# Linear attention of heads 0 and 1 interleaved with the gate projections, on other SBUF addresses, with the decays kept on chip

## The chip, the cores and the metric

One NeuronCore of a Trainium2 chip runs the whole kernel. The metric is the device time of one execution, in microseconds (us). An execution is also profiled; its trace gives the start and the length of every instruction on the engines: PE (matrix multiply; PEld is its weight load), DVE (vector), ACT (activation), POOL (GpSimd) and SP, whose queue issues nearly all DMAs here.

## The reference

A two-layer backbone over 256 context tokens and 1024 latent tokens, 1024 wide. Layer 0 is attention. Layer 1, where the change lies, runs two mixers side by side on the same normalized input `h`, and a SwiGLU block after them:

```python
q, k, v, g, lr, zg, zx = split(h @ w_in)              # 4 heads: q, k 64 wide, v 128 wide; g 512; zg, zx 512
log_a = log_sigmoid(lr @ gate_w + gate_b) / 16        # one decay for each head, key channel and direction
# linear attention, forward and backward in time, context first and then latent:
#   S <- exp(sum of log_a) * S + (k decayed to the block's end)^T v
#   o =  (q decayed from the block's start) S  +  the products inside the block
y_gla = rms_norm(o_forward + o_backward) * silu(g)    # g is the output gate
y_lru = (gated linear recurrence of conv(zx), both directions) * gelu(zg)
x = x + gate1 * (concat(y_gla, y_lru) @ w_out)
```

## The kernel before

All projections are transposed: 128 output channels on the partitions, tokens on the free axis in three chunks of 256, 512 and 512 (the first is the context). A product in float32 is made of three matmuls of split operands, so a 128-wide projection of all 1280 tokens is 72 matmuls on PE (8 blocks of the input, 3 products, 3 chunks). The code is written in program order; a planner with its own cost model puts each engine's instructions into one fixed order, near to program order, in which it lets ready work fill gaps that it foresees. On the chip each engine and the SP queue work that list strictly in order. Memory is handed out from pools that grow from the left or from the right end of SBUF; a tile that takes over the place of an older one waits until everything that uses the older tile is done.

`layer1` (L1679) runs a list of steps, `L1A` and then `L1B` (L54, L55). A letter is a kind of step and the digit the head or the group of 128 channels:

- `z` (`proj_zg`, L1348), `k` (`proj_t`, keys and queries of one head, 64 rows each), `x` (`proj_t` of the recurrence's input), `v` (`proj_v`, L1517, values, turned token-major by PE transposes L1527; its last chunk is turned in a later step) and `g` (`proj_g`, L1488, output gates of latent tokens, two chunks of 24 matmuls, then a Tanh on ACT, L1494, and a product on DVE, L1495). Their results go to DRAM through a ring of four tiles, `st`.
- `l` (`lru`, L1364): the recurrence of one group: convolution and gelu, 24 gate matmuls (L1390), activations, and scans on DVE (L1404, L1407, L1408). Its tile `ti` has one buffer.
- `a` (`gla_gates`, L1430): 6 small matmuls (L1438), Abs, Exp and Ln on ACT (L1440 to L1442) and the log decay `z` on DVE (L1443), which is stored to DRAM as `dz`.
- `p` (`gla_prep`, L1446): for each of the three chunks it loads `z` (L1461), keys over queries and queries over keys (L1457 to L1459), takes running sums `c` of `z` in blocks of 128 tokens (L1464, DVE), and makes from Exps of differences the decayed keys (POOL, L1479 and L1480, 64 rows each) and, for latent chunks, the decayed queries (DVE, L1484 and L1485, 64 rows each). Its tiles have one buffer, so a chunk's loads wait for the chunk before. `c`, the second sum `v` and both products go to DRAM.

When all steps are done, the pools of layer 1 and the one of `h` close, and the linear attention begins in the place of `h`, at the left end. For each head `gla_states` (L1551) loads decayed keys and values, makes the states of 8 blocks (PE transposes L1565, products L1571, a chain of 16 updates on DVE, L1583), and `gla_half` (L1586) does the first 512 latent tokens in 7 levels: two differences on POOL (L1620, L1621), an Exp on ACT (L1622), three products on DVE (two `kx` of 64 rows, L1627, and `qx`, L1628), 4 products on PE (L1632) and a masked copy on DVE (L1634). Then come the output products (L1639, L1640), a norm and the product with the gate. `gla_setup` (L1541) loads the masks and clears seven tiles for head 0. `out1` (L1666), the output projection, two rounds of 96 matmuls for the half of the input that comes from the recurrence, stands behind head 2 and behind head 3 in program order; its input (`y1_load`) and the residual tiles `x` are loaded behind head 0. The other 512 tokens of each head come later, inside the SwiGLU block.

Of the kernel before, what the change touches and what calls it, by code (L numbers as in the profile page):

```python
# [53 lines left out]
L1A = ops("z0 k0 l0 z1 k1 a0 l1 a1 z2 k2 a2 l2 a3")  # L54
L1B = ops("x3 z3 p0 k3 l3 p1 v0 p2 v1 v2 p3 v3 g0 g1 g2 g3")  # L55
# [84 lines left out]
class Trunk:  # L140
# [1000 lines left out]
    def layer0(self):  # L1141
# [165 lines left out]
        return h2, h2x, l1x  # L1307
# [8 lines left out]
    def proj(self, m, h, chunks, name):  # L1316
        w = self.wload(self.a["w1"][m], f"w1_{m}")
        for ci in chunks:
            cn = CH[ci][1]
            pt = self.psum(f"{name}{m}_{ci}", BANKS)  # L1320
            self.mm3(pt[:, 0:cn], w, h[ci], KT, lambda k: (slice(None), slice(k * P, (k + 1) * P)), lambda k: (slice(None), k))
            yield ci, pt[:, 0:cn]
# [107 lines left out]
    def gla_gates(self, pool, m):  # L1430

        nc = self.nc
        z = pool.tile([P, NTOK], F32, tag="pz", bufs=1, name=f"pz{m}")
        e = pool.tile([P, NTOK], F32, tag="pe", bufs=1, name=f"pe{m}")
# [9 lines left out]
        nc.sync.dma_start(self.dz[m], z)  # L1444

    def gla_prep(self, pool, m):  # L1446

        nc = self.nc
        for ci, (c0, cn) in enumerate(CH):
# [3 lines left out]
            def tl(tag, bufs=1):  # L1453
                return pool.tile([P, 512], F32, tag=tag, bufs=bufs, name=f"{tag}{nm}")[:, 0:cn]

            kq, qk = tl("pkq"), tl("pqk")
            nc.sync.dma_start(kq, self.dkq[m][:, sl])  # L1457
            nc.sync.dma_start(qk[0:64], self.dkq[m][64:128, sl])
            nc.sync.dma_start(qk[64:128], self.dkq[m][0:64, sl])  # L1459
            z, c, e = tl("pz"), tl("pc"), tl("pf")  # L1460
            nc.sync.dma_start(z, self.dz[m][:, sl])  # L1461
# [12 lines left out]
            ea, eb = e, tl("pb")  # L1474
            nc.gpsimd.tensor_tensor(v3(eb), ends.unsqueeze(2).to_broadcast([P, nt, P]), v3(z), op=ALU.subtract)
            nc.scalar.activation(ea, z, AF.Exp, scale=1.0 / 16)
            nc.scalar.activation(eb, eb, AF.Exp, scale=1.0 / 16)
            kh = tl("pk")
            nc.gpsimd.tensor_tensor(kh[0:64], kq[0:64], eb[0:64], op=ALU.mult)  # L1479
            nc.gpsimd.tensor_tensor(kh[64:128], qk[64:128], ea[64:128], op=ALU.mult)  # L1480
            nc.sync.dma_start(self.dkt[m][:, sl], kh)
            if ci:
                qh = c
                nc.vector.tensor_tensor(qh[0:64], qk[0:64], ea[0:64], op=ALU.mult)  # L1484
                nc.vector.tensor_tensor(qh[64:128], kq[64:128], eb[64:128], op=ALU.mult)  # L1485
                nc.sync.dma_start(self.dqh[m][:, c0 - C:c0 - C + cn], qh)

    def proj_g(self, h, pool, m):  # L1488

        nc = self.nc  # L1490
        for ci, pt in self.proj(4 + m, h, (1, 2), "g"):
# [4 lines left out]
            nc.sync.dma_start(self.dsg[m][:, c0:c0 + 512], st)  # L1496

# [19 lines left out]
    def proj_v(self, h, pool, m):  # L1517
# [4 lines left out]
        def turn(f, ci):  # L1522
# [7 lines left out]
            nc.sync.dma_start(self.dv[:, t0:t0 + nt, m * P:(m + 1) * P], st[:, 0:cn].rearrange("p (t c) -> p t c", c=P))  # L1530
# [10 lines left out]
    def gla_setup(self, pool):  # L1541
# [7 lines left out]
        self.st = {(h, 1): pool.tile([P, 4, P], F32, name=f"S1{h}") for h in range(4)}  # L1549

    def gla_states(self, pool, h, setup=None):  # L1551

        nc = self.nc
        kh = pool.tile([P, NTOK], F32, tag="kh", bufs=1, name=f"kh{h}")
        nc.sync.dma_start(kh, self.dkt[h])
        vh = pool.tile([P, 10, P], F32, tag="vs", bufs=2, name=f"vs{h}")
        nc.sync.dma_start(vh, self.dv[:, :, h * P:(h + 1) * P])
        if setup:
            setup()
        dec = self.dec[:, h]  # L1560
        u = []
        for g, (t0, tn) in enumerate(((0, 4), (4, 4), (8, 2))):
            pt = self.psum(f"kt{h}_{g}", "bb")
            for j in range(tn):
                nc.tensor.transpose(pt[:, j * P:(j + 1) * P], kh[:, (t0 + j) * P:(t0 + j + 1) * P], self.ident)  # L1565
            kt = pool.tile([P, 512], F32, tag="kt", bufs=2, name=f"kt{h}_{g}")
            self.evac(kt[:, 0:tn * P], pt[:, 0:tn * P])
            pu = self.psum(f"pu{h}_{g}")
            for j in range(tn):
                t = t0 + j  # L1570
                nc.tensor.matmul(pu[:, j * P:(j + 1) * P], kt[:, j * P:(j + 1) * P], vh[:, t], start=True, stop=True)  # L1571
                u.append(pu[:, j * P:(j + 1) * P])
# [13 lines left out]
    def gla_half(self, pool, h, half, tags="bbc"):  # L1586
# [18 lines left out]
        nc.sync.dma_start(vh, self.dv[:, 2 + half * 4:6 + half * 4, h * P:(h + 1) * P])  # L1605
# [73 lines left out]
    def layer1(self, h, h2x, l1):  # L1679
# [3 lines left out]
        self.dv = self.dp.tile([P, 10, 512], F32, name="dv")  # L1683
# [5 lines left out]
        self.dz = [self.dp.tile([P, NTOK], F32, name=f"dz{m}") for m in range(4)]  # L1689
# [5 lines left out]
        lp = lx.enter_context(self.pool("l1", "right"))  # L1695
        later = []

        def stages(todo, pp):
            for op, m in todo:
                turn = None  # L1700
# [317 lines left out]
```

## Time and profile before

| | us |
|---|---|
| median of 3 runs | 3202.02 |
| lowest and highest | 3200.45, 3204.18 |
| the profiled execution | 3202.41 |
| its span, first to last instruction | 3200.6 |

The span is the part of an execution that the trace shows; 1.8 us of the profiled execution lie around it. PE is busy 2927.1 us, DVE 2143.7, ACT 1278.9 and POOL 1258.3. Matmuls overlap one another, so that a busy PE is not yet a PE at its peak.

### The profile page before, as it was taken

The numbers are of one execution on the slowest core, as the hardware profiler recorded it, in microseconds if no ns is written. First come the engines' busy times: TensorE is split into PE (matmuls) and PEld (weight loads), VectorE is DVE, ScalarE is ACT, GpSimd is POOL, SyncE is SP. The second block draws the span as 40 slices with busy tenths as digits, with TensorE's granted clock in tenths as the row PEclk, the third lists the DMA queues.
The fourth block names the chain that finished last, engine by engine and source line by source line (L and its number), as shares of the span: only waits on it lengthen the run. The fifth ranks groups of instructions, "written<-read, shape, count | busy, mean of one in ns | idle before, by whom it ended". The sixth has DMA issues, their size and how long they took to land. (4 is left out here: it accounts for less than half of the span.)

```text
span 3200.6 us, 40905 instructions
## 1 busy us (share of the span) xinstructions
PE 2927.1 (91%) x14936; PEld 2396.7 (75%) x14936; DVE 2143.7 (67%) x3621; ACT 1278.9 (40%) x1971; POOL 1258.3 (39%) x741
## 2 busy tenths in 40 slices
PE   7998899998979999999989999886889999999997
PEld 5986677876768888888877766665667777787876
DVE  5598878885786555556687456647867665655487
ACT  4311655653442222324443367422333332333343
POOL 2333432332243333235445322444545434343455
PEclk9999999998989999999999999997989999999999
DMA  6576433315424444447423322567323233222452
GB/s 247 176 241 202 114 91 100 90 30 189 159 85 153 151 151 154 140 148 283 145 83 112 109 79 85 172 185 227 123 80 106 76 105 91 94 102 100 148 191 99
DMA packets 217193, 433.31 MB, mean 135 GB/s; under 512 B 23392, under 2 KB 91744, under 8 KB 216736
## 3 DMA queue, kind: packets, MB, share of 16 engines
q1 hardware_dynamic: 212384, 413.93, 40.3%
q10 hardware_dynamic: 4608, 16.78, 1.8%
q8 instruction: 117, 1.92, 0.2%
q14 instruction: 84, 0.69, 0.1%
HBM read 323.01 MB, written 107.61 MB: 135 GB/s over the span
## 5 line engine op out<-in xcount | busy, mean ns | idle before, releaser
L264 DVE SCALAR_TENSOR_TENSOR adaw<-adaw,cr 128x1024 f32<-128x1024 f32 x96 | 140.8, 1466 | 88.9 <-DMA adaw<-adat 88.7
L764 POOL TENSOR_TENSOR l_fx<-r_fin,h_fx 128x1024 fp32r<-128x1024 f32 x36 | 88.7, 2463 | 264.1 <-ACT h_fx L763 264.1
L764 POOL TENSOR_TENSOR l_fw<-r_fin,h_fw 128x1024 fp32r<-128x1024 f32 x36 | 87.4, 2428 | 168.0 <-ACT h_fw L763 148.3
L538 POOL TENSOR_SCALAR s_d<-s_d,cf_d 128x1280 f32<-128x1280 f32 (+1 forms) x40 | 46.6, 1164 | 248.3 <-DVE nb_d L525 63.6
L518 PE MATMUL ps_d<-kd,q 128*128 128x512 f32 (+1 forms) x416 | 116.5, 387 | 18.5 <-DVE s_d L520 13.4
L200 POOL TENSOR_TENSOR l_w<-r_w,h_w 128x1024 fp32r<-128x1024 f32 x33 | 85.0, 2578 | 95.0 <-ACT h_w L199 85.0
L520 DVE TENSOR_SCALAR_CACHE_REDUCE s_d<-ps_d 128x512 f32<-128x512 f32 (+1 forms) x208 | 117.1, 580 | 6.4 <-PE ps_d L518 5.1
L876 DVE TENSOR_TENSOR r_fin<-r_fin,r_fin 128x512 f32<-128x512 f32 x36 | 24.9, 692 | 132.1 <-POOL l_fx L764 131.9
L364 PE MATMUL pq<-hhi,h_w 128*128 128x512 f32 (+1 forms) x312 | 111.1, 356 | 1.5 <-DVE yl L435 1.5
L364 PE MATMUL pq<-hlo,h_w 128*128 128x512 f32 (+1 forms) x312 | 112.1, 359 | 0.0
L364 PE MATMUL pq<-hhi,l_w 128*128 128x512 f32 (+1 forms) x312 | 111.3, 357 | 0.0
L1632 PE MATMUL pg<-qx,kx 128*128 128x128 f32 x448 | 73.8, 318 | 31.0 <-DVE qx L1628 30.3
L539 POOL TENSOR_TENSOR s_d<-s_d,s_d 128x1280 f32<-128x1280 f32 (+1 forms) x40 | 99.7, 2493 | 3.3
L531 ACT ACTIVATE s_d<-s_d,nb_d 128x1280 f32<-128x1280 f32 (+1 forms) x80 | 94.5, 1183 | 14.5 <-DVE nb_d L526 8.8
L962 POOL TENSOR_TENSOR bl<-r_b,bh 128x1024 fp32r<-128x1024 f32 (+2 forms) x32 | 65.5, 2055 | 86.4 <-ACT bh L961 83.9
L1632 PEld LDWEIGHTS pg<-qx,kx 128*128 128x128 f32 x448 | 66.3, 224 | 41.6 <-issue 25.5
L518 PEld LDWEIGHTS ps_d<-kd,q 128*128 128x128 f32 x416 | 68.4, 194 | 34.6 <-DVE s_d L520 20.2
L962 POOL TENSOR_TENSOR bl_0t<-r_b0t,bh_0t 128x1024 fp32r<-128x1024 f32 (+1 forms) x24 | 70.0, 2924 | 61.3 <-ACT bh_0t L961 61.3
L432 POOL TENSOR_TENSOR rsh<-rsh,rope 128x512 f32<-128x512 f32 x26 | 41.3, 1590 | 133.4 <-DVE rsh L429 95.2
L364 PE MATMUL pd<-bh,h_fo 128*128 128x512 f32 (+1 forms) x228 | 84.7, 373 | 5.0 <-DVE xz L1018 2.7
L814 ACT ACTIVATE et<-es 128x512 f32<-128x512 f32 x54 | 34.0, 631 | 137.1 <-DVE es L887 68.4
L328 DVE TENSOR_TENSOR nacc<-nacc,nsq 128x512 f32<-128x512 f32 (+1 forms) x77 | 75.3, 981 | 20.0 <-ACT nsq L327 17.9
(625 smaller groups left out, 10405.4 us busy)
## 6 DMA issues: line engine op xcount, KB each, us to landing
r_fin<-fin SPq DMA_DIRECT2D x104, 512.0 KB, 3.6
adaw<-adat SPq DMA_DIRECT2D x64, 512.0 KB, 3.7
q<-dq SPq DMA_DIRECT2D x160, 128.0 KB, 3.0
r_w<-w SPq DMA_DIRECT2D x33, 512.0 KB, 3.8
adaw<-adat ACTq DMA_DIRECT2D x32, 512.0 KB, 4.8
r_wo<-wo SPq DMA_DIRECT2D x32, 512.0 KB, 3.8
w<-fo SPq DMA_DIRECT2D x32, 512.0 KB, 6.6
dbt<-et SPq DMA_DIRECT2D x44, 256.0 KB, 2.5
```

Of the source, the lines that this page charges most:

```text
L200: eng.tensor_tensor(lo, raw, hi.bitcast(F32), op=ALU.subtract)
L264: nc.vector.scalar_tensor_tensor(o, w, 1.0, cs[v], op0=ALU.mult, op1=ALU.mult, accum_out=self.adac[l][:, m, v:v + 1])
L328: nc.vector.tensor_tensor(acc, acc, sq, op=ALU.add)
L364: nc.tensor.matmul(out, w[wi][wsl(k)], x[xi][xsl(k)], start=(first and k == 0 and i == 0), stop=(last and k == nk - 1 and i == 2), skip_gr ...
L518: nc.tensor.matmul(pt[:, 0:kn], q[:, m, ab, j * P:(j + 1) * P], kt[:, m, k0:k0 + kn], start=(ab == 0), stop=(ab == 1))
L520: nc.vector.tensor_scalar(s[m][:, k0:k0 + kn], pt[:, 0:kn], 1.0, None, op0=ALU.mult, op1=ALU.max, accum_out=mx[:, m, c:c + 1])
L531: nc.scalar.activation(s[m][:, 0:nk * P], s[m][:, 0:nk * P], AF.Exp, bias=nb[:, m:m + 1], scale=SC, accum_out=sm[:, m:m + 1])
L538: nc.gpsimd.tensor_scalar(a1, a1, cf, 0.0, op0=ALU.mult, op1=ALU.add)
L539: nc.gpsimd.tensor_tensor(a0, a0, a1, op=ALU.add)
L764: eng.tensor_tensor(lo[:, 0:n], raw[:, 0:n], hi[:, 0:n].bitcast(F32), op=ALU.subtract)
L962: eng.tensor_tensor(lo[:, 0:n], raw, hi[:, 0:n].bitcast(F32), op=ALU.subtract)
L1632: nc.tensor.matmul(pg[:, b], kx[:, b], qx[:, b], start=True, stop=True)
```

## The change

1. One list `L1` takes the place of `L1A` and `L1B`: values and preparation (`v`, `p`) stand between the recurrences, and the `g` steps leave the list. The ring `st` and the tiles of `a` and `p` get pools at the left (`stp`, `pp`).
2. `a` keeps `z` in SBUF (`self.z`), in one buffer until its `p` has read it; `dz` is gone, its store and its loads too. The scratch tile of `a` is now the recurrence's `ti`.
3. `p` loads keys twice and queries twice (forward and backward rows), and forms both exponents as 128-row tiles whose halves hold the two directions; decayed keys and decayed queries are one Exp and one product of all 128 rows each. The decayed keys take a slot of the ring `st`. The second sum is stored as two halves of 64 rows.
4. Values lie in DRAM as one tensor for each head.
5. The working tiles of the linear attention (`gp`, `gh`) move to the right end, where the recurrence's tiles were; heads 0 and 1 take their decayed keys, values and states from four tiles in the pool of `h` that held the normalized context tokens (`WT[2][0:4]`). `h` thus stays, and the `g` steps are interleaved with heads 0 and 1: three steps of the heads, then one chunk of a gate.
6. The residual tiles and the later pools move to the left; `x` and the first `y1_load` come behind head 1, and `out1` behind heads 2 and 3.

```diff
-L1A = ops("z0 k0 l0 z1 k1 a0 l1 a1 z2 k2 a2 l2 a3")
-L1B = ops("x3 z3 p0 k3 l3 p1 v0 p2 v1 v2 p3 v3 g0 g1 g2 g3")
+L1 = ops("z0 k0 l0 k1 z1 v0 l1 a0 p0 z2 k2 v1 l2 a1 p1 x3 z3 k3 v2 l3 a2 p2 v3 a3 p3")
...
-    def gla_gates(self, pool, m):
+    def gla_gates(self, pool, lp, m):
-        z = pool.tile([P, NTOK], F32, tag="pz", bufs=1, name=f"pz{m}")
-        e = pool.tile([P, NTOK], F32, tag="pe", bufs=1, name=f"pe{m}")
+        self.z = z = pool.tile([P, NTOK], F32, tag="pz", bufs=1, name=f"pz{m}")
+        e = lp.tile([P, NTOK], F32, tag="ti", bufs=1, name=f"pe{m}")
...
-        nc.sync.dma_start(self.dz[m], z)
...
+            kk, qq = tl("pkq"), tl("pqk")
+            for i, t in enumerate((kk, qq)):
+                if i == 0 or ci:
+                    for r in (lo, hi):
+                        nc.sync.dma_start(t[r], self.dkq[m][64 * i:64 * i + 64, sl])
+            z, c = self.z[:, sl], tl("pc")
...
+            ka, qa = tl("pf"), tl("pb")
+            nc.vector.tensor_tensor(ka[hi], c[hi], z[hi], op=ALU.subtract)
+            nc.scalar.activation(qa[lo], c[lo], AF.Copy)
...
-            nc.gpsimd.tensor_tensor(kh[0:64], kq[0:64], eb[0:64], op=ALU.mult)
-            nc.gpsimd.tensor_tensor(kh[64:128], qk[64:128], ea[64:128], op=ALU.mult)
+            for r, t, v in ((lo, ka, c), (hi, qa, ka)):
+                nc.gpsimd.tensor_tensor(v3(t[r]), ends[r].unsqueeze(2).to_broadcast([64, nt, P]), v3(v[r]), op=ALU.subtract)
+            kh, qh = tl("st", sp, 4), c
+            nc.scalar.activation(kh, ka, AF.Exp, scale=1.0 / 16)
+            nc.gpsimd.tensor_tensor(kh, kh, kk, op=ALU.mult)
             nc.sync.dma_start(self.dkt[m][:, sl], kh)
             if ci:
-                nc.vector.tensor_tensor(qh[0:64], qk[0:64], ea[0:64], op=ALU.mult)
-                nc.vector.tensor_tensor(qh[64:128], kq[64:128], eb[64:128], op=ALU.mult)
+                nc.scalar.activation(qh, qa, AF.Exp, scale=1.0 / 16)
+                nc.vector.tensor_tensor(qh, qh, qq, op=ALU.mult)
...
     def proj_g(self, h, pool, m):
-        for ci, pt in self.proj(4 + m, h, (1, 2), "g"):
+        for ci, pt in self.proj(4 + m, h, (1, 2), "g", "ad"):
...
             nc.sync.dma_start(self.dsg[m][:, c0:c0 + 512], st)
+            yield
...
+        gp, gh = [gx.enter_context(self.pool(n, "right")) for n in ("gp", "gh")]
+        gates = chain(*[self.proj_g(h, stp, m) for m in range(4)])
+        next(gates)
+        for turn in later:
+            turn()
+        def heads():
+            for hd in range(2):
+                t = [hb.tile([P, 1024], F32, tag=tag, bufs=1, name=f"gl{hd}{i}") for i, tag in enumerate(WT[2][0:4])]
+                self.gla_states(((t[0], t[3][:, 0:256]), (v3(t[1]), v3(t[3][:, 256:512])), (t[2][:, 0:512], t[2][:, 512:1024]),
+                                 self.st[3, 1] if hd else v3(t[3][:, 512:1024])), hd, None if hd else lambda: self.gla_setup(gp))
+                yield from self.gla_half(gh, hd, 0)
+        weave(heads(), gates, 3)
         h2x.close()
...
+            y = self.y1_load(yp, 1, 1)
+            for ci in (1, 2):
+                c0 = CH[ci][0] - C
+                for k in range(KT):
+                    nc.sync.dma_start(x[ci][:, k], self.dx[:, k, c0:c0 + 512])
+            for hd in (2, 3):
+                self.gla_states(self.gla_tiles(pool, hd), hd)
                 run(self.gla_half(gh, hd, 0))
+                run(self.out1(y, x, 1, hd - 1, "ad"))
+                if hd == 2:
                     y = self.y1_load(yp, 1, 2)
```

## Rows read from the trace of the kernel before

**Rows 1.** Stretches: length, busy PE, PEld, DVE, ACT, POOL (instructions), clock, DMA share, GB/s.
```profile
1839.50:2010.50 171.00, 160.17 (x650) 116.60 (x649) 102.51 (x85) 114.34 (x132) 44.65 (x28) 0.94 0.26 89
2010.50:2107.50 97.00, 76.91 (x349) 60.83 (x348) 54.62 (x58) 42.02 (x69) 46.47 (x30) 0.89 0.55 171
2107.50:2151.80 44.30, 44.30 (x199) 36.35 (x197) 23.81 (x30) 14.65 (x28) 20.52 (x15) 1.00 0.60 188
2151.80:2163.30 11.50, 0.04 (x2) 0.05 (x1) 5.54 (x5) 2.15 (x4) 8.70 (x10) 0.66 0.72 241
2163.30:2308.70 145.40, 112.52 (x609) 94.87 (x610) 116.96 (x216) 47.96 (x74) 74.23 (x76) 0.82 0.57 175
2308.70:2334.00 25.30, 22.29 (x97) 17.72 (x96) 14.59 (x23) 8.61 (x12) 13.64 (x11) 0.87 0.42 132
```

**Rows 2.** Timeline of PE, last gate to first level: start, length, instruction, [idle before, releaser].
```profile
2151.43 0.39 PE L364 MATMUL g<-h,h_w 128*128 128x512 f32 x1
2163.28 2.51 PE L1565 MATMUL kt<-ident,kh 128*128 128x128 f32 x10 [11.46 <-DMA kh<-dkt]
2176.51 0.77 PE L1632 MATMUL pg<-qx,kx 128*128 128x128 f32 x2 [5.48 <-DVE qx L1628]
```

**Rows 3.** Timeline of the SP queue, and of POOL, at the same place.
```profile
2157.14 0.41 SPq L1496 DMA_DIRECT2D dsg<-stg  x1
2157.65 0.38 SPq L1555 DMA_DIRECT2D kh<-dkt  x1
2164.27 0.38 SPq L1595 DMA_DIRECT2D C<-dc  x1
...
2170.90 0.62 POOL L1620 TENSOR_TENSOR D<-C,V 128x256 f32<-128x256 f32 x1 [10.40 <-DMA C<-dc]
```

**Rows 4.** Waits from 2151.8 to 2334: who waited for whom, us, times, longest.
```profile
POOL D L1620 <- DVE qx L1628: 32.9, 12, 8.4
PE pg L1632 <- DVE qx L1628: 28.5, 18, 5.5
```

**Rows 5.** Waits from 1839.5 to 2151.8.
```profile
DVE pc L1464 <- DMA pz<-dz: 45.0, 9, 8.5
PE vt L1527 <- ACT vf L1534: 13.9, 4, 5.0
```

**Rows 6.** Timeline of PE: projection k3, then the gate matmuls of recurrence 3.
```profile
1996.69 0.28 PE L364 MATMUL kq<-h,h_w 128*128 128x256 f32 x1
...
2010.47 4.46 PE L1390 MATMUL lg<-xr,r_lg 128*128 128x256 f32 x12
2021.10 6.81 PE L1390 MATMUL lg<-xr,r_lg 128*128 128x256 f32 x12 [6.17 <-DVE stkq L1314]
```

**Rows 7.** Timelines: first gate matmul of recurrence 0; last scans of recurrences 0 and 3.
```profile
1864.21 8.75 PE L1390 MATMUL lg<-xr,r_lg 128*128 128x256 f32 x24
1891.59 2.34 DVE L1408 TENSOR_TENSOR_SCAN lq<-av,lq,ti 128x1024 f32<-128x1024 f32 x1
2048.56 2.64 DVE L1408 TENSOR_TENSOR_SCAN lq<-av,lq,ti 128x1024 f32<-128x1024 f32 x1
```

**Rows 8.** Timelines of ACT and DVE: the decay of head 0.
```profile
1904.75 1.28 ACT L1440 ACTIVATE pe<-pz 128x1280 f32<-128x1280 f32 x1
1910.96 1.49 DVE L1443 SCALAR_TENSOR_TENSOR pz<-pz,pe 128x1280 f32<-128x1280 f32 x1 [7.05 <-ACT pe L1442]
```

**Rows 9.** Lines one by one: count, shortest/median/longest ns, first and last start.
```profile
L1464 DVE TENSOR_TENSOR_SCAN pc<-ones,pz x40: 391/398/2360, 2006.6 to 2147.1; 128x128 f32<-128x128 f32 x40
L1479 POOL TENSOR_TENSOR pk<-pkq,pb x12: 717/1604/2604, 2010.7 to 2150.9; 64x512 f32<-64x512 f32 x8, 64x256 f32<-64x256 f32 x4
L1484 DVE TENSOR_TENSOR pc<-pqk,pf x8: 683/1712/2786, 2016.9 to 2151.2; 64x512 f32<-64x512 f32 x8
L1485 DVE TENSOR_TENSOR pc<-pkq,pb x8: 1648/1669/4037, 2018.7 to 2152.8; 64x512 f32<-64x512 f32 x8
L1628 DVE TENSOR_TENSOR qx<-qk,D x30: 669/693/2108, 2175.7 to 2311.8; 128x512 f32<-128x512 f32 x30
```

More of the change, by code (lines that the diff above doesn't have):

```diff
@@ L1306, in layer0 @@
         fx.close()
-        return h2, h2x, l1x
+        return h2, hb, h2x, l1x
     def evac(self, dst, src, i=1):
@@ L1564, in gla_states @@
             for j in range(tn):
-                nc.tensor.transpose(pt[:, j * P:(j + 1) * P], kh[:, (t0 + j) * P:(t0 + j + 1) * P], self.ident)
-            kt = pool.tile([P, 512], F32, tag="kt", bufs=2, name=f"kt{h}_{g}")
+                nc.tensor.transpose(pt[:, j * P:(j + 1) * P], key(t0 + j), self.ident)
+            kt = kts[g % 2]
             self.evac(kt[:, 0:tn * P], pt[:, 0:tn * P])
@@ L1682, in layer1 @@
         self.dy = [self.dp.tile([P, T], F32, name=f"dy{i}") for i in range(8)]
-        self.dv = self.dp.tile([P, 10, 512], F32, name="dv")
+        self.dv = [self.dp.tile([P, 10, P], F32, name=f"dv{i}") for i in range(4)]
         self.dc = [self.dp.tile([P, T], F32, name=f"dc{i}") for i in range(4)]
@@ L1722, in layer1 @@
-        with self.pool("pg") as pp:
-            stages(L1A, pp)
-        stages(L1B, l1.enter_context(self.pool("pp")))
-        l1.close()
+        for op, m in L1:
+            turn = None
+            if op == "x":
+                self.proj_t(h, stp, 12 + m, self.dzx[m], f"zx{m}")
+            elif op == "k":
+                self.proj_t(h, stp, m, self.dkq[m], f"kq{m}")
+            elif op == "z":
+                self.proj_zg(h, lp, m)
+            elif op == "v":
+                turn = self.proj_v(h, stp, m)
+            elif op == "a":
+                self.gla_gates(pp, lp, m)
+            elif op == "p":
+                self.gla_prep(pp, stp, m)
+            else:
+                self.lru(lp, m)
+            if op in "vkxz" and later:
+                later.pop()()
+            if turn:
+                later.append(turn)
@@ L1726, in layer1 @@
+        weave(heads(), gates, 3)
         h2x.close()
-        lx.close()
-        ctx0, gx = ExitStack(), ExitStack()
-        gp, gh = [gx.enter_context(self.pool(n)) for n in ("gp", "gh")]
-        xp = ctx0.enter_context(self.pool("xp1", "right"))
+        ctx0 = ExitStack()
+        xp = ctx0.enter_context(self.pool("xp1"))
         def xtiles(name):
@@ L1760, in layer1 @@
         prs, ps = {}, {}
-        with self.pool("o1", "right") as pool:
+        with self.pool("o1") as pool:
             run(self.out1(self.y1_load(pool, 0, 1, sc), x, 0, 1, BANKS))
```

121 lines of the change are left out of this document (42 added, 79 removed).

## The prediction

> **What bounds the kernel now.** I read the page's busy shares first: PE is busy 2927 of 3200.6 us, so time is lost only where PE stands idle or runs at the lower of its two clock levels. A table of stretches then finds the place [rows 1]. In layer 1 up to the end of the gates (1839.5 to 2151.8) PE idles 10.8 us in the first stretch (171.0 less 160.2), 20.1 in the second and nothing in the third; the mean granted clock of 0.94 in the first means that it ran at 1.2 instead of 2.4 GHz for about 12% of the time, which costs 6% of 171, some 10 us. Then come 11.5 us with no PE work at all. The linear attention with the interleaved output projection (145.4 us to the last head's output products) has PE busy 112.5 us at a clock of 0.82, and a tail of 25.3 us.
>
> The timeline of PE names the empty 11.5 us: the last gate matmul starts at 2151.43, the first transpose of head 0 at 2163.28, released by the load of the decayed keys, and the first level's product follows at 2176.51 [rows 2]. In the SP queue that load stands behind a gate store that waits for its data and goes at 2157.14; the last tile the levels need, `C`, is issued at 2164.27, and POOL begins on it at 2170.90 [rows 3]. After that the waits go round in a ring: POOL's differences wait 32.9 us for DVE's `qx` and PE's products 28.5 us for the same line [rows 4]. So the heads are bound by DVE and POOL, and PE has room there. Before that, preparation is a slow chain: DVE waits 45.0 us in 9 waits for `z` to come back from DRAM, and PE 13.9 us for the values' copies [rows 5].
>
> **The change part by part.** The sum follows one path, from the first gate matmul of recurrence 3 (2010.47, [rows 6]) to the first level's product of head 0 (2176.51), 166.0 us now; what follows that product is shifted with it.
>
> *Where recurrence 3 starts.* Three value projections move ahead of it. One projection of 1280 tokens takes 13.8 us (1996.69 to 2010.47, [rows 6]), so +41.4 us, and some 3 us for the 30 transposes that go along (estimate: each is a quarter of a 512-column product, 30 x 0.1). Against that, this longer PE work lies between recurrences that now make PE wait. Of the 21 us lost in the first stretch (10.8 idle, 10 of clock) I take back 10; the ends are 0 and 21. Start: 2010.5 + 44.4 - 10 = 2044.9.
>
> *From there to head 0.* The levels' tiles now lie where the recurrence's tiles were. The scratch of `a3` is `ti`, so tiles over `ti` wait for `a3`; `a3` cannot put its `z` down until `p2` has read the last piece of `a2`'s, and `a2` needs `ti` from recurrence 3. Nothing of this was a chain before. Its links:
> - recurrence 3, first gate matmul to the last scan's end: 29.7 us for recurrence 0 (1864.21 to 1893.93), 40.7 for recurrence 3 (2010.47 to 2051.20), which ran among preparation steps [rows 7]. I take 34.
> - `a2`: Abs starts at 1904.75 and the DVE step ends at 1912.45 [rows 8]: 7.7.
> - `p2` until its third chunk has read `z`: the 12 chunks of the four heads start from 2006.6 to 2147.1 [rows 9], so with the third chunk's four scans 12.4 apart. Nine waits on the loads of `z` make 45.0 [rows 5], 5.0 each, and go. The queries' products become one of 128 rows instead of two of 64 (1.71 + 1.67 us by their medians); the same 512 columns on 128 rows take 0.69 at best in `qx` [rows 9], so rows cost nothing and 1.7 to 2.7 us of DVE go per latent chunk, 14 to 22 in all, hidden beside the rest of the chunk's chain. POOL keeps three operations a chunk. Ends 7.4 and 12.4; I take 9, so two spacings and 2 us: 20.
> - `a3`: 7.7, and 1.8 for writing `z` (an estimate from 1.28 us for the same columns in one ACT instruction): 9.5.
> - the load of `C` to POOL's start, 6.6 (2164.27 to 2170.90, [rows 3]), and on to PE's first product, 5.6 (2176.51, [rows 2]): 12.2.
>
> Sum 34 + 7.7 + 20 + 9.5 + 12.2 = 83.4, so the first product comes at 2128.3 instead of 2176.5: **-48.2 us**. PE has 8.8 (gate matmuls, [rows 7]) + 13.8 (`v3`) + 4.8 (an estimate for the small matmuls of `a2` and `a3`) + 44.3 (the `g` steps, [rows 1]) = 71.7 us of work in these 83.4, so the gates are hidden here and the empty 11.5 us are within what goes. That also means that most of the gates run ahead of the heads rather than woven into them.
>
> *Beside head 0.* `p3` is still to do. On DVE it is 10 scans of 0.40 and six operations of 0.7 [rows 9], 8 us; on POOL 9 operations at 0.7 to 1.6, some 10. Heads are bound by those two engines. Below 0 is excluded, since it is added work there; 20 if both add up; I take **+10**.
>
> A row bears on how the two add: L1485, 64 rows, never took under 1648 ns, while `qx` with twice the rows has 669 [rows 9]; its partner on POOL, L1479, runs at the same time. The Trainium skill ("SBUF — State Buffer", section "SBUF: two separate sides") says why: a DVE instruction with two SBUF inputs and a POOL instruction that reads SBUF take turns, each for its whole length. By that rule p3 costs head 0 all 20 us and the forecast would be 10 us later; it stays inside the range below.
>
> *The rest of the heads.* From the first product to the end of the tail it is 2334.0 - 2176.5 = 157.5 us, and I leave it so. The same 14 DVE and POOL operations per two levels bound it. The states of heads 1 and 3 now load into tiles that the head before still uses for its output products; their late updates have a whole head's levels as cover (price without it: one load, some 6 us by the 6.6 of `C`). `x` and `y` load 5 MB behind head 1 instead of head 0; they are wanted by `out1` behind head 2, some 35 us later.
>
> *Without price.* `dz` takes 4 stores and 12 loads from the SP queue; the doubled rows and the halves of the second sum put some back (22 issues per head become 21). Contiguous values only shorten stores. The mirrored pools change addresses after 2334, where no long wait is named.
>
> Sum: 3202.4 of the profiled execution - 48.2 + 10 = **3164 us**; the median of the runs shown is 3202.0, 0.4 below that execution, so it is the same against it.
>
> **The rivals.**
> 1. *Heads start early.* If the tiles of the first levels happen not to lie over `ti`, head 0 starts when PE is through `v3` (2044.9 + 8.8 + 13.8 + 4.8 = 2072) with its loads already in, first product at 2078, and the weave does what it says. Then -98.5, and `p2` and `p3` both run beside heads 0 and 1, +20 to +25: 3127. For it: PE has idle room of 33 us and half clock in the heads. Against: the recurrence's pool is about as large as what replaces it.
> 2. *The hand-over stalls instead.* The tiles of heads 2 and 3, `x` and `y` take the place of `h`, so they wait for the last gate, and 20 loads stand in the same SP queue. If a gap like the one that goes opens between heads 1 and 2 (11.5 us) and one load shows per state (6.6), the gain is 20 us: 3182.
> 3. *The ring of four stalls PE: slower.* The decayed keys of `p0`, `p1` and `p2` now take slots of `st`, and copies of the projections behind them wait for those slots. If a projection has to wait two chunk spacings of 12.4 less what seven PSUM banks let PE run ahead (half that), PE loses 15 us at each of the three places, 45 in all, and 3164 becomes 3209. It decides from about 13 us per place. For it: already now PE stood 6.17 us because a copy was late [rows 6], and 13.9 behind copies of values [rows 5]. Against: between a `p` and the third use of the ring lie 11 to 25 us of other PE work.
> 4. *Hidden anyway.* Heads slow down by what they start earlier: 3202.
>
> **How the numbers follow.** The forecast has 0.48, rival 1 0.18, rival 2 0.18, rival 3 0.09, rival 4 0.07. 0.2% (6 us) is about what can be told from no change. Faster: 0.48 + 0.18 + 0.18 = 0.84; same 0.07; slower 0.09. The bounds of the likeliest: -11 (idle recovered), -4 (recurrence), -3 (chunks), -10 (p3) give 3136, and +10, +7, +7, +10 give 3198; its own range is 3143 to 3186. The range over all, 3122 to 3198, takes in the two faster rivals and leaves out rivals 3 and 4 and a few per cent at the lower end.
>
> **What would show it.** Right: no wait of the scans on a load of `z`; PE without the 11.5 us; gates nearly done when the first level's product starts, 80 to 85 us after recurrence 3; prepared chunks 9 us apart. Wrong: levels that start before `a3`'s decay is done (rival 1); long waits on `x`, keys or values after the last gate (rival 2); projections' copies waiting for the store of decayed keys (rival 3); a stretch of the heads longer than 157.5 us by more than 20.

## The result and the profile after

The changed kernel takes 3222.8 us (median of 4 runs, 3219.5 to 3223.7) against 3201.2 before (4 runs, 3195.0 to 3204.2): ratio 1.0068, 95% interval 1.005 to 1.0085. It is 0.7% slower, where I forecast 1.2% faster. The profiled execution took 3223.0 us, with a span of 3221.2.

The stretches of the changed kernel, cut where those of before were cut [rows 1] (length, busy PE, PEld, DVE, ACT, POOL, clock, DMA share, GB/s):

```profile
1835.40:2058.40 223.00, 194.02 (x880) 152.46 (x879) 127.83 (x116) 116.26 (x148) 73.42 (x47) 0.93 0.32 103
2058.40:2163.40 105.00, 66.93 (x258) 47.76 (x257) 48.66 (x71) 55.14 (x78) 39.73 (x36) 0.76 0.47 149
2163.40:2327.30 163.90, 129.24 (x669) 105.25 (x668) 114.75 (x201) 50.59 (x76) 77.98 (x75) 0.85 0.46 147
2327.30:2353.00 25.70, 22.23 (x97) 18.24 (x95) 14.04 (x21) 9.04 (x13) 13.88 (x11) 0.84 0.39 123
```

The first begins with the first gate projection `zg`, the second with recurrence 3's first gate matmul, the third with head 0's first level product, the fourth with the last head's output products. Against before: +52.0 (223.0 for 171.0), -61.0 (105.0 for 166.0), +31.7 (163.9 for 132.2) and +0.4 (25.7 for 25.3); the layer begins 4.1 us earlier and what follows is 1.6 longer. The sum is +20.6, the difference of the spans. So the chain in the middle did become shorter, by 61.0 of the 82.6 us that the prediction has for it (166.0 less 83.4), and its two neighbours lost 83.7, where I had 34.4 for the first and 10 for the second.

Where it went shows in four new idle times of PE, in one late load, and in a stop of the levels between heads 1 and 2 (shown at e4). The timeline of the changed kernel: PE, then DVE and ACT ahead of the first and the third, then the way from a3's decay to the first level's product (start, length, engine, instruction, [idle before, releaser]):

```profile
1964.26 0.79 PE L363 MATMUL pv<-h,h_w 128*128 128x512 f32 x1 [10.67 <-DVE stv L1313]
2030.82 0.80 PE L363 MATMUL kq<-h,h_w 128*128 128x512 f32 x1 [16.55 <-DVE stzx L1313]
2111.01 1.60 PE L1529 MATMUL vt<-ident,vf 128*128 128x128 f32 x6 [19.79 <-ACT vf L1536]
2146.08 1.22 PE L1584 MATMUL pu<-gl,gl 128*128 128x128 f32 x4 [12.78 <-DVE stg L1496]
...
1956.63 1.19 DVE L1486 TENSOR_TENSOR pc<-pc,pqk 128x512 f32<-128x512 f32 x1 [1.60 <-ACT pc L1485]
1961.39 1.37 DVE L1464 TENSOR_TENSOR_SCAN pc<-ones,pz 128x128 f32<-128x128 f32 x4 [3.57 <-DMA dqh<-pc]
1963.52 0.69 DVE L1313 COPY stv<-vt 128x512 f32<-128x512 f32 x1
...
2108.48 0.63 ACT L1469 ACTIVATE pb<-pc 64x512 f32<-64x512 f32 x1 [5.45 <-DVE pc L1464]
2110.05 0.63 ACT L1481 ACTIVATE st<-pf 128x512 f32<-128x512 f32 x1 [0.84 <-POOL pf L1479]
2110.59 0.85 ACT L1536 ACTIVATE vf<-pv 128x256 f32<-128x256 f32 x2
...
2122.27 1.49 DVE L1442 SCALAR_TENSOR_TENSOR pz<-pz,pe 128x1280 f32<-128x1280 f32 x1 [6.95 <-ACT pe L1441]
2148.07 0.32 SPq L1487 DMA_DIRECT2D dqh<-pc  x1
2153.08 0.43 SPq L1606 DMA_DIRECT2D C<-dc  x1
2157.38 0.62 POOL L1631 TENSOR_TENSOR D<-C,V 128x256 f32<-128x256 f32 x1 [10.76 <-DMA C<-dc]
2163.44 1.06 PE L1643 MATMUL pg<-qx,kx 128*128 128x128 f32 x8
```

Each of the four idle times (59.8 us together) ends with a copy out of the memory that PE writes (the last with the gate's product, which also frees a bank). The copy is not slow, and its data had long been there: the values whose copy runs on ACT at 2110.59 were finished on PE before 2087. It stands in its engine's list behind the last chunk of a preparation: copy, Exp, copy on ACT; product, scan, copy on DVE. And that chunk comes late, in part since its scans overwrite `pc`, from which the queries of the chunk before are still being stored (3.57 us here). The last five lines are the other loss: a3's decay is done at 2123.76, but head 0's `C` is issued at 2153.08, behind p3's last store of queries (2148.07), and the first product comes at 2163.44, 39.7 us after the decay. Only 10.76 us of these are POOL's wait for that load: until 2146.62 (2157.38 less 10.76) POOL itself was at p3, whose products stand ahead of head 0's first difference in its list.

The waits that answer to [rows 4, 5], the first from the stretch 1835.4 to 2163.4, the others from 2163.4 to 2353:

```profile
DVE pc L1464 <- DMA dqh<-pc: 14.9, 4, 4.9
...
POOL D L1631 <- DVE qx L1639: 51.5, 15, 21.4
PE pg L1643 <- DVE qx L1639: 19.6, 15, 4.0
```

The scans no longer wait for `z` (45.0 us before), but 14.9 for the store of queries. In the heads the ring of POOL and DVE is there still, but 21.4 of the 51.5 us are one wait, between heads 1 and 2. Last, two lines that answer to [rows 9]:

```profile
L1464 DVE TENSOR_TENSOR_SCAN pc<-ones,pz x40: 390/398/947, 1947.0 to 2142.1; 128x128 f32<-128x128 f32 x40
L1486 DVE TENSOR_TENSOR pc<-pc,pqk x8: 678/706/1612, 1956.6 to 2147.4; 128x512 f32<-128x512 f32 x8
```

The queries' product of 128 rows has a median of 0.71 us, in place of two of 1.71 and 1.67.

### The profile page after: what moved, and what is told of

Read it like the earlier page. It is cut to its first block, busy times and chain, and to the rows that moved or that the text cites. A ratio compares the mean times of both kernels' runs of the same rounds, so it can differ in the third digit from the quotient of the medians.

```text
span 3221.2 us, 40881 instructions
## 1 busy us (share of the span) xinstructions
PE 2923.6 (91%) x14936; PEld 2393.7 (74%) x14936; DVE 2130.3 (66%) x3613; ACT 1280.2 (40%) x1967; POOL 1251.5 (39%) x741
## 5 line engine op out<-in xcount | busy, mean ns | idle before, releaser
L763 POOL TENSOR_TENSOR l_fw<-r_fin,h_fw 128x1024 fp32r<-128x1024 f32 x36 | 86.9, 2413 | 168.5 <-ACT h_fw L762 157.7
L1631 POOL TENSOR_TENSOR D<-C,V 128x256 f32<-128x256 f32 x56 | 47.8, 854 | 108.0 <-DVE qx L1639 78.9
L199 POOL TENSOR_TENSOR l_wo<-r_wo,h_wo 128x1024 fp32r<-128x1024 f32 x24 | 59.8, 2491 | 76.3 <-ACT h_wo L198 76.3
L1643 PE MATMUL pg<-qx,kx 128*128 128x128 f32 x448 | 68.2, 303 | 22.2 <-DVE qx L1639 21.6
```

Source lines behind the costliest of these rows:

```text
L199: eng.tensor_tensor(lo, raw, hi.bitcast(F32), op=ALU.subtract)
L763: eng.tensor_tensor(lo[:, 0:n], raw[:, 0:n], hi[:, 0:n].bitcast(F32), op=ALU.subtract)
L1631: nc.gpsimd.tensor_tensor(w4(d)[:, :, 0], r, w4(v)[:, :, 0], op=ALU.subtract)
L1643: nc.tensor.matmul(pg[:, b], kx[:, b], qx[:, b], start=True, stop=True)
```

## The experiments

Thirteen kernels, each timed against the kernel before on the same chip (one chip for each of the groups e1 to e4, e5 to e8, e9 to e12 and e13). The three middle columns are read from each kernel's own timeline: from the first `zg` matmul to recurrence 3's first gate matmul, from there to head 0's first level product, and from there to the end of the last head's output products. (The third of the stretches above ends where these products start, so it is 2.6 us shorter: 163.9 for 166.5.)

| kernel | to recurrence 3 | to first product | heads | ratio to before, 95% |
|---|---|---|---|---|
| before | 170.9 | 166.0 | 134.2 | 1 |
| changed | 223.0 | 105.1 | 166.5 | 1.0068, 1.005 to 1.0085 |
| e1 queries | 212.2 | 98.9 | 160.2 | 1.0017, 1.0006 to 1.0029 |
| e2 keys | 200.0 | 102.0 | 161.4 | 0.9983, 0.9969 to 0.9996 |
| e3 late | 202.1 | 112.8 | 162.7 | 1.0033, 1.0019 to 1.0047 |
| e4 gates first | 222.2 | 117.5 | 138.2 | 1.0037, 1.0022 to 1.0051 |
| e5 queries, keys | 200.1 | 103.7 | 163.1 | 0.9996, 0.9982 to 1.001 |
| e6 heads as before | 222.0 | 118.3 | 147.9 | 1.0064, 1.0047 to 1.0082 |
| e7 queries, keys, heads | 200.5 | 109.0 | 141.6 | 0.9942, 0.9926 to 0.9959 |
| e8 width alone | 166.3 | 156.8 | 134.3 | 0.9966, 0.9951 to 0.998 |
| e9 p3 behind head 0 | 222.5 | 80.5 | 174.6 | 1.0043, 1.0029 to 1.0058 |
| e10 small heads | 222.1 | 101.3 | 158.4 | 1.0032, 1.0018 to 1.0045 |
| e11 keys, p3 behind | 200.7 | 81.2 | 168.5 | 0.9949, 0.9937 to 0.9961 |
| e12 and gates first | 200.0 | 85.6 | 154.3 | 0.9918, 0.9905 to 0.9931 |
| e13 slot short | 219.1 | 100.8 | 161.7 | 1.0059, 1.0042 to 1.0076 |

**e1: queries leave `pc`.**

```diff
-                nc.vector.tensor_tensor(qh, qh, qq, op=ALU.mult)
-                nc.sync.dma_start(self.dqh[m][:, dst], qh)
+                nc.vector.tensor_tensor(qq, qh, qq, op=ALU.mult)
+                nc.sync.dma_start(self.dqh[m][:, dst], qq)
```

> Decayed queries are written over the loaded queries (tile pqk) instead of over the running sums (tile pc), so the next chunk's scans need not wait until the store of the queries has landed. Theory A (in-order engines: copies of the projections stand on DVE and ACT behind a preparation chunk whose scan waits for that store): the four waits of the scans on dqh<-pc (14.9 us) go to 0, PE's four stalls (10.7, 16.6, 19.8, 12.8 us) lose about 3 to 5 us each, and the time falls by 8 to 15 us from 3222.8, to about 3211. Theory B (the ring st: decayed keys hold slots that the copies need): the waits of the scans may go, but the stalls stay within 2 us each and the time within 4 us of 3222.8.

Measured: 0.5% below the changed kernel. The waits on the store are gone (the releasers of the scans' idle time in e1, and PE's four idle times):

```profile
L1464 DVE TENSOR_TENSOR_SCAN pc<-ones,pz x40: 391/400/2495, 1952.0 to 2129.3; 128x128 f32<-128x128 f32 x40
  ACT dec L1477: 5.7, 3
  POOL pb L1479: 0.5, 1
```

```profile
1967.74 0.80 PE L363 MATMUL pv<-h,h_w 128*128 128x512 f32 x1 [9.17 <-DVE stv L1313]
2024.95 0.79 PE L363 MATMUL kq<-h,h_w 128*128 128x512 f32 x1 [5.91 <-DVE stzx L1313]
2102.05 1.60 PE L1529 MATMUL vt<-ident,vf 128*128 128x128 f32 x6 [16.61 <-ACT vf L1536]
2133.21 1.22 PE L1584 MATMUL pu<-gl,gl 128*128 128x128 f32 x4 [8.88 <-DVE stg L1496]
```

The stalls are 40.6 us in place of 59.8, 4.8 less each on average (1.5 at the first, 10.6 at the second): theory A's gain, a little above its range in time (some 16 us for 8 to 15). But they are still there.

**e2: keys leave the ring.**

```diff
-            kh, qh = tl("st", sp, 4), c
+            kh, qh = ka, c
             nc.scalar.activation(kh, ka, AF.Exp, scale=1.0 / 16)
-            nc.gpsimd.tensor_tensor(kh, kh, kk, op=ALU.mult)
-            nc.sync.dma_start(self.dkt[m][:, sl], kh)
+            nc.gpsimd.tensor_tensor(kk, kh, kk, op=ALU.mult)
+            nc.sync.dma_start(self.dkt[m][:, sl], kk)
```

> Decayed keys leave the ring st: their Exp is taken in place (tile pf) and their product is written over the loaded keys (tile pkq). Theory B (ring): the four stalls of PE, 59.8 us together, fall below 5 us each and the time falls by 25 to 45 us, to 3180 to 3198. Theory A (in-order engines behind the preparation chain): the stalls stay, 50 to 70 us together, and the time stays within 6 us of 3222.8.

Measured: 0.85% (27 us) below the changed kernel, recurrence 3 23 us earlier. PE's idle times at the three places of the projections, and ACT at the first, in e2:

```profile
1959.11 0.69 PE L1529 MATMUL vt<-ident,vf 128*128 128x128 f32 x2 [4.07 <-ACT vf L1536]
2030.69 0.44 PE L1529 MATMUL vt<-ident,vf 128*128 128x128 f32 x2 [2.15 <-ACT vf L1536]
2080.38 0.66 PE L1578 MATMUL kt<-ident,gl 128*128 128x128 f32 x4 [4.58 <-DVE stv L1313]
...
1958.69 0.36 ACT L1536 ACTIVATE vf<-pv 128x256 f32<-128x256 f32 x1
1964.13 0.63 ACT L1469 ACTIVATE pb<-pc 64x512 f32<-64x512 f32 x1 [5.08 <-DVE pc L1464]
```

The copy of values now stands ahead of the last chunk's copy of sums. Theory B holds for these three places. The fourth stall stayed (12.67 us at 2110.13, now behind DVE's state updates), which B did not foresee.

**e13: how the ring does it.** Keys take a slot in the same order, and give it back without a store.

```diff
-            nc.gpsimd.tensor_tensor(kh, kh, kk, op=ALU.mult)
-            nc.sync.dma_start(self.dkt[m][:, sl], kh)
+            nc.gpsimd.tensor_tensor(kk, kh, kk, op=ALU.mult)
+            nc.sync.dma_start(self.dkt[m][:, sl], kk)
```

> Decayed keys still take a slot of the ring st for their Exp, but the product is written over the loaded keys and stored from there, so a slot is free 1 to 3 us earlier, without the wait for a store to land. If copies lose their time by waiting for such stores: stalls as in the run with the keys outside the ring (4, 2 and 5 us), ratio 0.998 to 1.001. If they lose it because a slot that passes from keys to a copy puts the copy behind the preparation chunk in the order of ACT and DVE (the order of ACT's copies vf behind the Exps of preparation 2 is the same as in the changed kernel): the stalls of about 10, 16 and 20 us stay, ratio 1.004 to 1.008.

```profile
1961.27 0.80 PE L363 MATMUL pv<-h,h_w 128*128 128x512 f32 x1 [10.07 <-DVE stv L1313]
2024.26 0.80 PE L363 MATMUL kq<-h,h_w 128*128 128x512 f32 x1 [12.32 <-DVE stzx L1313]
2103.16 1.60 PE L1529 MATMUL vt<-ident,vf 128*128 128x128 f32 x6 [18.15 <-ACT vf L1536]
```

The idle times of PE in e13 stay, though the second is 4.2 us shorter, and so does the time (1.0059, where e2 has 0.9983). So copies lose little of their time waiting for stores of keys. e13 and e2 differ in the slot alone, and with it in the lists: at the third place the copy of values follows the Exp of the last chunk on ACT in the changed kernel (2110.59 behind 2110.05) and in e13 (2102.74 behind 2102.20), while in e2 (2059.13) it runs ahead of the whole preparation (first copy of sums at 2074.86). A slot that passes from keys to a copy puts the copy behind that chunk's instructions in the lists of ACT and DVE, and there it waits for whatever the chunk waits for.

**e5: both.** The edits of e1 and e2 together.

> Both edits of the two runs before in one kernel: decayed queries over the loaded queries, decayed keys outside the ring. Taken alone they stood 0.5% and 0.85% (16 and 27 us) below the changed kernel. If the ring and the scans' wait for the queries' store are two delays one after the other, they add: about 43 us below it, ratio to the kernel before 0.993 to 0.996, no PE stall above 5 us before the first transpose of head 0. If both only reach the same next limit (the chain recurrence 3, a2, p2, a3, p3), the ratio is that of the keys alone, 0.997 to 0.999.

They don't add: 0.9996 against 0.9983 with the keys alone, intervals overlapping, and recurrence 3 begins at 200 either way. As I read it, a late scan delays no projection once their copies stand ahead of the chunk.

**e3: preparations later in the list.**

```diff
-L1 = ops("z0 k0 l0 k1 z1 v0 l1 a0 p0 z2 k2 v1 l2 a1 p1 x3 z3 k3 v2 l3 a2 p2 v3 a3 p3")
+L1 = ops("z0 k0 l0 k1 z1 v0 l1 a0 z2 k2 v1 p0 l2 a1 x3 z3 k3 v2 p1 l3 a2 v3 p2 a3 p3")
```

> Only the list of steps is changed: each preparation p stands behind the projections and values that followed it (z0 k0 l0 k1 z1 v0 l1 a0 z2 k2 v1 p0 l2 a1 x3 z3 k3 v2 p1 l3 a2 v3 p2 a3 p3). Theory A: the copies of these projections now stand ahead of the preparation on DVE and ACT; the stalls of 10.7 and 16.6 us shrink below 5 us and recurrence 3 starts some 20 us earlier than 2058.4; p2 still delays a3, so the first level's product comes 10 to 20 us earlier than 2163.4; time 3203 to 3213. If instead the order is not the cause (theory B, ring, or a slower preparation by itself), the time stays within 5 us of 3222.8 or rises.

Measured 1.0033, 11 us below the changed kernel, recurrence 3 20.9 us earlier, and 7.7 given back on the way to the first product. For the copies ahead of recurrence 3 the program order does what leaving the ring does; behind it PE now stands idle for 21.2 and 16.7 us. Since a later preparation also takes its slots later, e3 doesn't tell the slot from the place in the list; e13 does.

**e4: gates first.**

```diff
-        weave(heads(), gates, 3)
+        run(gates)
+        run(heads())
```

> All eight chunks of the gates stand ahead of heads 0 and 1 in program order instead of between their steps. If the weave fills idle time of PE in the heads (as the change is meant to), taking it away costs the 24 us of gate matmuls that now run after the first level's product, less the idle time that they fill before it: 8 to 20 us slower, 3231 to 3243. If the gates only lengthen the heads by their own length (PE's idle time in the stretch of the heads is 34.7 us against 27.2 before, so nothing was filled), the time stays within 5 us of 3222.8.

Neither: taking the weave away makes it faster by 0.3%. The stretches of e4 before and from the first product, then the changed kernel's from the first product to the same end:

```profile
2057.10:2174.60 117.50, 86.08 (x354) 63.25 (x352) 52.28 (x69) 61.83 (x87) 48.77 (x42) 0.85 0.51 160
2174.60:2312.90 138.30, 106.59 (x589) 89.01 (x589) 108.73 (x205) 44.44 (x68) 69.12 (x69) 0.86 0.47 151
...
2163.40:2330.00 166.60, 131.94 (x685) 107.94 (x684) 117.39 (x205) 50.60 (x77) 79.47 (x77) 0.85 0.45 144
```

The gates inside the heads are 96 matmuls and 25.3 us of PE (131.9 - 106.6), and the heads with them are 28.3 us longer; ahead of the heads they cost 12.5 (117.5 for 105.0). PE is idle for about as long in both (34.7 and 31.7), as if the gates had filled nothing. But the time from head to head says something else. From the first product to each head's product with the norm (L1660), heads 0 and 1 together take 71.4 us in the changed kernel and 69.1 in e4, where 27 matmuls of `out1` run there instead; head 2 takes 62.0 and 39.5, head 3 45.2 and 43.3. So beside heads 0 and 1 the gates did fit into idle time, and the loss lies in head 2. There the changed kernel's timeline and its SP queue's wait for the last gate (L1672 loads the input of `out1`), then e4's timeline, show:

```profile
2234.85 0.39 PE L363 MATMUL g<-h,h_w 128*128 128x512 f32 x1
2235.04 0.80 SPq L1672 DMA_DIRECT2D y<-dy  x2
2253.21 0.32 SPq L1564 DMA_DIRECT2D gl<-dkt  x1
2271.01 0.84 POOL L1631 TENSOR_TENSOR D<-C,V 128x256 f32<-128x256 f32 x1 [21.35 <-DVE qx L1639]
...
SPq L1672 <- PE g L363: 6.2, 1, 6.2
...
2225.01 0.32 SPq L1564 DMA_DIRECT2D gl<-dkt  x1
2251.47 0.73 POOL L1631 TENSOR_TENSOR D<-C,V 128x256 f32<-128x256 f32 x1 [5.61 <-DVE qx L1639]
```

With the weave `h` is in use until 2234.85, and the tiles of `y`, `x` and head 2 lie in its place. Their loads start behind that gate; the keys of head 2 go behind 16 loads of `x`, 89.8 us after the first product (50.4 in e4, beside head 1), and the levels stand still for 21.35 us, in which DVE's list has updates of `x` and of head 2's states that need those loads. All kernels with the weave have such a stop, of 20.5 to 21.5 us; where the gates come first (e4, e6, e7, e12) no wait of the levels inside the heads is over 5.6. No run moves these loads alone.

**e6: heads in the order of before.** Only this part of the program is exchanged: all gates, `h` closed, then

```diff
+            for hd in range(4):
+                self.gla_states(self.gla_tiles(pool, hd), hd, None if hd else lambda: self.gla_setup(gp))
+                run(self.gla_half(gh, hd, 0))
+                if hd == 0:
+                    y = self.y1_load(yp, 1, 1)
...
+                if hd == HO:
+                    run(self.out1(y, x, 1, 1, "ad"))
```

> The changed kernel up to the last preparation; then all gates, then h is closed, and the four heads run in the program order of the kernel before (x and y loaded behind head 0, out1 behind heads 2 and 3), on the changed kernel's addresses. Theory H (in the kernel before the idle time of PE in heads 0 and 1 was already filled by out1; the woven gates took its place, and out1, whose tiles lie where h was, is pushed behind the last gate): from the first level's product to the last matmul of out1 it takes 155 to 162 us as before instead of 190, the first product comes at about 2175, and the ratio to before is 0.998 to 1.003 (16 to 28 us below the changed kernel). Rival (the heads are longer because of the tiles with one buffer or the addresses): the stretch stays over 175 us and the time over 1.004.

Theory H falls. By its own measure, to the last matmul of `out1`, e6 comes near it with 163.7 us (187.2 in the changed kernel), but e4, which leaves `out1` where the change put it, takes 159.6; the stretch of the table is 147.9, 9.7 longer than in e4, and the time is that of the changed kernel. That `out1` was pushed back is not why the heads are long; that the gates are done before the heads is what e4 and e6 share. **e7** adds the edits of e1 and e2 to it:

> Queries and keys as in the two-edit kernel, and the heads in the program order of before. If the causes are independent: first level's product near 2150, 158 us for the heads, ratio to before 0.988 to 0.993. If the gates must be hidden behind the preparation and are not, 0.994 to 1.000.

0.9942, with 109.0 and 141.6 for the two last stretches: the lower end of the second case. Beside e5 (103.7 and 163.1) the heads gain 21.5 and the way to them loses 5.3.

**e8: one part of the change alone, in the kernel before.** Products of 128 rows, halves loaded as in the change; keys in a tile of their own.

```diff
-            nc.gpsimd.tensor_tensor(kh[0:64], kq[0:64], eb[0:64], op=ALU.mult)
-            nc.gpsimd.tensor_tensor(kh[64:128], qk[64:128], ea[64:128], op=ALU.mult)
+            nc.scalar.activation(kh, ka, AF.Exp, scale=1.0 / 16)
+            nc.gpsimd.tensor_tensor(kh, kh, kk, op=ALU.mult)
...
-                nc.vector.tensor_tensor(qh[0:64], qk[0:64], ea[0:64], op=ALU.mult)
-                nc.vector.tensor_tensor(qh[64:128], kq[64:128], eb[64:128], op=ALU.mult)
+                nc.scalar.activation(qh, qa, AF.Exp, scale=1.0 / 16)
+                nc.vector.tensor_tensor(qh, qh, qq, op=ALU.mult)
```

> The kernel before with one part of the change alone: decayed keys and queries as 128-row products, keys and queries loaded by halves; order, z through DRAM and heads as before, keys in their own tile. The prediction had 1.7 to 2.7 us of DVE per latent chunk go, hidden beside the chain of the chunk: within 6 us of before (ratio 0.998 to 1.002). If preparation bounds the start of head 0, its twelve chunks are 1 to 1.5 us closer and the ratio is 0.994 to 0.997. If the two loads more per head and the Exp of its own hurt, 1.002 or more.

0.9966. Its scans span 121.0 us in place of 140.5 [rows 9], 1.8 a chunk:

```profile
L1466 DVE TENSOR_TENSOR_SCAN pc<-ones,pz x40: 393/400/2559, 2000.4 to 2121.4; 128x128 f32<-128x128 f32 x40
```

So this part is worth something in the kernel before: what I took for hidden is, at least in part, on the path. It also changes the keys on POOL, the Exps and the loads, and e8 doesn't tell these from the queries' 1.7 to 2.7 us.

**e9 and e10: p3 behind head 0.** e10 gives five tiles of the heads one buffer (the first two pairs of lines, and `vh`, `o`, `sg` likewise), which makes the room that e9 needs; e9 also moves p3.

```diff
-            t = pool.tile([P, 512], F32, tag=tag, bufs=2, name=f"{tag}{nm}")
+            t = pool.tile([P, 512], F32, tag=tag, bufs=1 if tag == "qh" else 2, name=f"{tag}{nm}")
...
-        am = pool.tile([P, 512], F32, tag="A", bufs=2, name=f"A{nm}")
+        am = pool.tile([P, 512], F32, tag="A", bufs=1, name=f"A{nm}")
...
-L1 = ops("z0 k0 l0 k1 z1 v0 l1 a0 p0 z2 k2 v1 l2 a1 p1 x3 z3 k3 v2 l3 a2 p2 v3 a3 p3")
+L1 = ops("z0 k0 l0 k1 z1 v0 l1 a0 p0 z2 k2 v1 l2 a1 p1 x3 z3 k3 v2 l3 a2 p2 v3 a3")
...
                 yield from self.gla_half(gh, hd, 0)
+                if hd == 0:
+                    self.gla_prep(pp, stp, 3)
+                    l1.close()
```

> The changed kernel with preparation 3 moved behind head 0 (its working tiles stay open until then) and, to make room, five tiles of the heads (qh, vh, A, o, sg) with one buffer instead of two, so that the heads' tiles no longer reach down to the preparation's. Theory C (in the changed kernel head 0's loads stand in the SP queue behind the stores of preparation 3, and that is why its first level's product comes 39.6 us after a3's decay is done and not 12.2): the first level's product comes 12 to 16 us after a3's decay, 24 to 28 us earlier than in the changed kernel, and the scans of preparation 3 run beside heads 0 and 1. If it then costs what the prediction took (+10), the time is 10 to 18 us below the changed kernel, ratio 1.001 to 1.004. If preparation 3 costs the heads all that was gained, the ratio stays within 0.0015 of 1.0068.

> Control: the changed kernel with the five tiles of the heads with one buffer alone; preparation 3 stays ahead of head 0. Theory C: head 0's running sums are still loaded behind the last stores of preparation 3, the first product stays within 5 us of the changed kernel's, the ratio within 0.002 of 1.0068. Rival D (not the queue but the addresses hold head 0 back, since the heads' tiles reach into those of the preparation): the first product comes 20 us earlier without moving the preparation, ratio 1.001 to 1.004.

e9, then e10, from recurrence 3 to the first product and through the heads:

```profile
2067.50:2147.90 80.40, 58.20 (x242) 40.75 (x240) 42.83 (x61) 51.18 (x70) 31.12 (x29) 0.83 0.47 146
2147.90:2322.50 174.60, 134.92 (x702) 109.96 (x702) 124.61 (x213) 54.58 (x84) 87.71 (x82) 0.86 0.49 156
```

```profile
2055.90:2157.20 101.30, 61.77 (x239) 43.16 (x238) 48.10 (x69) 55.15 (x78) 39.22 (x35) 0.76 0.46 147
2157.20:2315.60 158.40, 129.47 (x703) 104.22 (x704) 115.08 (x205) 50.48 (x76) 78.98 (x75) 0.90 0.49 152
```

Theory C holds for the start: with most of p3 behind it the first product comes 80.4 us after recurrence 3 and 15.3 after a3's decay. (Moving p3 takes its stores out of the SP queue and its work out of the lists of POOL and DVE, so e9 doesn't tell these two apart.) But the heads then take 16.2 us more than the control's, so little is left: 1.0043 and 1.0032 can't be told apart. D falls, since the control's first product comes only 3.7 us earlier (101.3 for 105.0). Its time is another matter: 1.0032, where C had 1.0068, through heads that are 8.1 us shorter (158.4 for 166.5). I did not expect that, and its cause is open.

**e11 and e12: the edits together.** e11 is e9 with the keys of e2; e12 has the gates first as well (`run(gates)`, then `run(heads())`).

> As the run with preparation 3 behind head 0, and decayed keys outside the ring st. The keys alone brought 0.85% against the changed kernel. If that and the queue are independent: another 20 to 27 us, ratio 0.992 to 0.996. If both run into the same limit (PE's own work between recurrence 3 and head 0, some 70 us): 0.996 to 0.999.

> As the run before it (keys outside the ring, preparation 3 behind head 0), with all gates ahead of heads 0 and 1 in program order. Gates first alone took 28 us from the heads and gave 12 back ahead of them. If that holds here too, the ratio falls by 0.004 to 0.006 against the run before it, to 0.987 to 0.992. If the gates now only delay a head 0 that could start, no change between the two.

0.9949, as with independent causes, then 0.9918: here too the gates are cheaper ahead of the heads, by 0.3%, and the stop of the levels between heads 1 and 2 (21.1 us in e11) is gone. e12 beats both kernels, by 0.8% and by 1.5% (0.9918 / 1.0068 = 0.985). Its stretch from recurrence 3 to the first product:

```profile
2035.80:2121.40 85.60, 79.00 (x324) 59.66 (x323) 47.32 (x51) 54.63 (x76) 39.38 (x35) 0.94 0.49 158
```

PE is idle for 6.6 us between recurrence 3 and the first product, against 38.1 in the changed kernel, and its granted clock there is 0.94 instead of 0.76. Beyond e8, which parts of the change make e12 faster than the kernel before was not separated.

## Why the prediction was wrong

The sum missed by 59, in three terms: 17.6 for recurrence 3, 21.6 for the chain, 21.7 for the heads; less 4.1 for the earlier start, and 2.0 behind.

*Where recurrence 3 starts.* I said 205.4 us after the first `zg` (2044.9 - 1839.5); it was 223.0. With keys outside the ring it is 200.0 (e2), so the three moved projections and the idle taken back were priced about right. What failed is this start, 17.6 us too early, by the dismissal of rival 3. Its "against", that 11 to 25 us of other PE work lie between a p and the third use of the ring, asked when a slot comes free. e13 shows that this is not the question: the slot fixes the copy's place in the list, and from there the copy pays for every wait of the preparation, the scans' wait for the queries' store among them, which I had not seen either (e1). Rival 3 gave 3209 with 45 us at three places; they measured 47.0 (10.67 + 16.55 + 19.79). That is luck: 15 a place doesn't follow from its own working (two spacings of 12.4 less half), its sign, copies that wait for a store of keys, makes 3.4 us in three waits, and the third place lies behind the start of recurrence 3.

*From there to head 0.* Recurrence 3 took 26.5 us (34 said), a2 8.9 (7.7), p2 15.3 (20), a3 14.6 (9.5): 65.3 of 71.2. The links before the last are 5.9 shorter in sum, with errors that offset each other. The last link failed, 39.7 in place of 12.2, since p3 is not beside head 0 but ahead of it: in POOL's list until 2146.62, and in the SP queue, where head 0's loads stand behind its stores, for the 10.8 us after that. I had asked for a row on when their tiles come free, and not for what stands ahead of them in the lists. With p3 out of the way the chain takes 80.4 (e9), 83.4 being the forecast.

*p3 beside head 0.* The +10 was in the wrong place, and small: where p3 does run beside the heads it costs 16.2 (e9 less e10), inside the bounds of 0 and 20. The rule of the Trainium skill that I weighed there ("SBUF — State Buffer", section "SBUF: two separate sides") gave 20, which is nearer; no run here shows that this rule is why.

*The rest of the heads.* I left them as they were, because 71.7 us of PE work, the gates among them, should fit in the 83.4 of the chain, and gave the late loads of `x` and `y` no price. The stalls took that room: 66.9 of PE work got done in 105.0, and half of the gates, 25.3 us, were left for the heads. Beside heads 0 and 1 they cost little (71.4 against 69.1 in e4), so the idle PE that I had read there as room (33 us, 145.4 less 112.5, [rows 1]) was in part room. But they kept `h` in use to their end, and the loads into its place stopped the levels for 21.35 us. This is rival 2, at the place that it names and near its price (11.5 + 6.6 = 18.1 us), to which I had given 0.18; it came on top of the other losses.

*Right:* no scan waits for a load of `z`; the empty 11.5 us between the last gate and head 0 are gone, though longer ones opened elsewhere; the queries' product at 0.7 us. That the last of these is hidden, so worth nothing, is put in doubt by e8.

## What to carry to other kernels

A ring of buffers handed out in program order is also an order for the engines: before a slow chain takes slots in a ring of quick copies, ask which copies will then be listed behind it, and what it waits for. For every load of the next stage, look at what stands ahead of it in the issuing queue, not only at when its tile comes free. Work that is moved into the idle time of an engine also keeps its operands' memory in use for longer: look up which loads go into that memory, and what waits for them.

## What the runs showed of the hardware

Taking away the scans' wait in e1 gave back part of it in another form. POOL's split of a weight tile and the scans there, in e1:

```profile
1962.23 2.79 POOL L199 TENSOR_TENSOR l_w<-r_w,h_w 128x1024 fp32r<-128x1024 f32 x1
1962.92 3.32 DVE L1464 TENSOR_TENSOR_SCAN pc<-ones,pz 128x128 f32<-128x128 f32 x4
```

and the first of those four scans by itself (count, shortest/median/longest ns):

```profile
L1464 DVE TENSOR_TENSOR_SCAN pc<-ones,pz x1: 2374/2374/2374, 1962.9 to 1962.9; 128x128 f32<-128x128 f32 x1
```

Four scans took 3.32 us where they take 1.37 alone (1961.39 in the changed kernel); the first began 0.7 us behind POOL's product, lasted 2.37 and ended 0.3 us behind that product's end (1965.02). A scan reads two SBUF tiles. The Trainium skill ("SBUF — State Buffer", section "SBUF: two separate sides") says that such a DVE instruction and a POOL instruction that reads SBUF exclude each other for the whole of the one that began first; this trace agrees.
